# Reordering the last part of the output product and the block loads behind it in a hybrid decoder layer

## The chip, the cores and the metric

One core of a Trainium2 chip runs the whole kernel. The metric is the device time in microseconds of that core for one execution. Five engines work from queues of their own, each in order: PE (matrix products, with its weight loads listed as PEld), DVE (vector operations), ACT (activations, copies and casts), POOL and SP (here used almost only to issue DMAs). An engine waits for another through semaphores.

## The reference, cut to what matters

One layer: a normalised input is projected; a branch of causal pooling and a branch of a state-space scan (SSD) are each multiplied by an output matrix, weighed by sigmoid gates and added; an MLP follows. The change touches the end of the SSD branch (`y_ssd`) and the start of the pooling branch.

```python
def mamba2_branch(z, xbc, dt_raw, conv_w, conv_b, dt_bias, a_log, d_skip, norm_w):
    ...
    y = ssd_chunked(xs, dt, a, b_mat, c_mat) + xs * d_skip[:, None]
    y = y.reshape(bsz, seqlen, D_INNER) * jax.nn.silu(z)
    yg = y.reshape(bsz, seqlen, SSM_GROUPS, D_INNER // SSM_GROUPS).astype(jnp.float32)
    yg = yg * lax.rsqrt(jnp.mean(yg * yg, axis=-1, keepdims=True) + EPS)
    return yg.reshape(bsz, seqlen, D_INNER).astype(z.dtype) * norm_w
...
        y_pool = pool_mixer(u_pool, pool_w_group[i], pool_scale[i]) @ w_pool_up[i]
        y_ssd = mamba2_branch(z, xbc, dt_raw, conv_w[i], conv_b[i], dt_bias[i], a_log[i],
                              d_skip[i], ssd_norm_w[i]) @ w_ssd_out[i]
        h = h + (gate_pool * y_pool + gate_ssd * y_ssd) @ w_o[i]
```

There are 512 tokens, a width of 1024, and 8 groups in the SSD branch with 256 channels each, so 16 slices of 128 channels go into `@ w_ssd_out`.

## The kernel before

**Numbers in two parts.** Every fp32 operand is split into a high part (a cast on ACT) and a low part (a subtraction on DVE), and a product is made of three: high by high, high by low, low by high (`mm3s`, lines 147, 148 and 150). Weights come as blocks of 128x1024: SP loads `raw`, ACT casts `whi`, DVE subtracts `wlo`. There are three `raw` buffers (a fourth here and there while the scan runs) and four each of `whi` and `wlo`, so the load of a block waits until DVE is done with the block three before. Blocks 56 to 67 are the ones that matter here.

**The end of the scan.** `ssd(g)` works through the eight groups. Its last steps for group 7 are: products `po` and `py`, the chain on DVE that makes `yt`, its square `sqg` on ACT (L707), the high part `qhg` (ACT, L331) and the low part `qlg` (DVE, L332) of the sum of squares, two column-sum products `png` on PE (L713, L714), the root `rs` on ACT (L716), reciprocals on DVE, and the split of the result into `yh` and `yl` (L725, L726). Beside it `out_part` runs, piece by piece, as a second generator: eight tiles `psp0` to `psp7` (one for each 128 output channels), each a product with slices 8 to 13 of y. Slices 12 and 13 come from group 6 and are late, so for tiles 0 and 1 they are taken apart (`late`, L884) and go over both tiles in turn. A finished tile is copied out of PSUM by ACT into one of two staging buffers (`sp`, L872), and POOL adds it to `acc_d` in memory by an accumulating DMA (L873). Tiles of `psp` and the pool pair's `pxx` share two PSUM buffers (`psum2`); `png`, `py`, `pz`, `po` and `psl` share four others (`psum1`).

**Behind it.** `pool_pair` makes eight products of the first pool pair from three weights (A, S, D) and a half one (B), with partial sums `pxx`, `py` and `pz` that ACT and DVE copy or add into `pu` between the products (L1012 to L1031). The weights S and D are sums of the raw blocks (`sm`, L986 to L991). Then the last part of the SSD output, slices 14 and 15 of y (group 7), comes in eight tiles `psl0` to `psl7` from two blocks (64 for tiles 0 to 3, 65 for 4 to 7, handed out by `units`), and DVE adds each to `acc` (L1065), which POOL has read back from `acc_d` (L1057). Block 66 holds the pool group's weights and block 67 a gate's; `pool_mix` and its products `pg` with `ph` and `pl` (L974, L975) follow.

**What sets the order.** The program is traced in this order, and a scheduler then places instructions on each engine by priority and readiness. `tc.high_priority(100)` moves what is traced inside it ahead; `tc.issue_after(i)` and the helper `after` keep what is traced inside behind instruction `i` on the same engine, without a semaphore. `block(behind, cast_behind)` gives a block's subtraction and its cast such a place.

## Time and profile before

| | us |
|---|---|
| median of 3 timed runs | 1001.3 (1001.02 to 1001.38) |
| the profiled execution's own time | 999.86 |
| its span, first to last instruction | 998.2 |
| busy time in the span: PE / PEld / DVE / ACT / POOL | 986.7 / 873.1 / 804.1 / 602.0 / 120.1 |

Busy time of PE is pipelined time, so 99% of the span does not say that PE could not be faster; it says that PE hardly ever stands still. Where it does stand still is to be read from the waits of PE and of its weight loads, and from the timeline around them. The `out_part` tiles run from about 430 to 474 us of the span, the first pool pair from 474 to 485, and the `psl` tiles from 485 to 496.

### The profile page before, as it was taken

Reading aid. Unit: us, or ns where it says so; the run is one execution under the profiler, and the core shown is the slowest. Engines: PE = TensorE matmul, PEld = TensorE weight load, DVE = VectorE, ACT = ScalarE, POOL = GpSimd, SP = SyncE. Lnnn points to the kernel's source line nnn. Section 1 sums busy time; section 2 is a strip of 40 time slices with the busy share of each in tenths; the row PEclk is TensorE's granted clock in tenths of the full one; section 3 lists DMA queues with packets and bytes.
Section 4 is the critical chain, followed back from the end, with each engine's and each line's share of the span. In section 5 each row is a group of like instructions: output and inputs, shape, how many; then the busy total and the mean of one; then the engine's idle time right before and its main releaser. Section 6 shows DMA issues by size and latency. Waiting matters only on the chain.

```text
span 998.2 us, 15676 instructions
## 1 busy us (share of the span) xinstructions
PE 986.7 (99%) x6035; PEld 873.1 (87%) x6035; DVE 804.1 (81%) x1162; ACT 602.0 (60%) x855; POOL 120.1 (12%) x216
## 2 busy tenths in 40 slices
PE   8999999999999999999999999999999999999997
PEld 7889998989889999978899888888889999999986
DVE  7978997879845888978789657877988888888885
ACT  8657839495924658574345443378666656656654
POOL 0011321211212212223200022100000000000000
PEclk9999999999999999999999999999999999999999
DMA  7274967667897848678813777864164454464332
GB/s 255 84 257 147 271 196 215 188 194 210 227 274 238 242 124 268 218 159 173 284 67 128 255 247 186 261 177 155 64 190 148 151 187 150 147 188 149 129 106 85
DMA packets 61803, 184.52 MB, mean 185 GB/s; under 512 B 7072, under 2 KB 8416, under 8 KB 60704
## 3 DMA queue, kind: packets, MB, share of 16 engines
q1 hardware_dynamic: 39456, 109.00, 32.9%
q0 software_dynamic: 18240, 67.51, 26.3%
q10 hardware_dynamic: 4032, 7.00, 1.9%
q8 instruction: 47, 0.77, 0.3%
q14 instruction: 28, 0.23, 0.1%
HBM read 173.13 MB, written 58.59 MB: 232 GB/s over the span
## 4 chain that ended last, share of the span: by engine, by line
PE 93%; ACT 3%; DMA 2%; DVE 1%; issue 1%; SPq 0%; ACTq 0%; DVEq 0%
PE px L1468 8%; PE px L216 8%; PE alpha L1536 6%; PE pz L216 6%; PE px L1471 4%; PE px L219 4%; PE alpha L1539 3%; PE pgp L216 3%; PE pz L219 3%; PE pgs L216 3%; PE py L695 2%; PE pqx L510 2%; DMA raw<-in_w 2%; PE pso L147 1%; PE pgp L219 1%; PE wo_alpha L1229 1%
## 5 line engine op out<-in xcount | busy, mean ns | idle before, releaser
L114 DVE TENSOR_TENSOR wlo<-raw,whi 128x1024 fp32r<-128x1024 f32 (+2 forms) x88 | 102.1, 1172 | 37.7 <-ACT whi L112 21.7
L112 ACT CAST whi<-raw 128x1024 fp32r<-128x1024 f32 (+2 forms) x88 | 87.2, 1011 | 67.8 <-PE pso L148 15.3
L216 PE MATMUL px<-uh,whi 128*128 128x264 f32 (+1 forms) x320 | 80.9, 291 | 0.0
L219 PE MATMUL px<-ul,whi 128*128 128x264 f32 (+1 forms) x320 | 78.8, 285 | 0.0
L1243 DVE TENSOR_TENSOR ht<-ht,alpha 128x1024 f32<-128x1024 f32 x35 | 42.7, 1219 | 29.1 <-PE alpha L1536 29.1
L1160 ACT CAST shi<-rawf 128x1024 fp32r<-128x1024 f32 x42 | 44.2, 1053 | 28.7 <-PE alpha L1539 18.2
L216 PEld LDWEIGHTS px<-uh,whi 128*128 128x128 f32 x320 | 60.4, 189 | 0.9 <-issue 0.7
L219 PEld LDWEIGHTS px<-ul,whi 128*128 128x128 f32 x320 | 60.2, 188 | 0.4 <-issue 0.2
L1536 PE MATMUL alpha<-shi,hh 128*128 128x512 f32 x140 | 55.2, 394 | 0.0
L1539 PE MATMUL alpha<-shi,hl 128*128 128x512 f32 x140 | 54.7, 391 | 0.0
L1161 DVE TENSOR_TENSOR slo<-rawf,shi 128x1024 fp32r<-128x1024 f32 x42 | 51.2, 1219 | 0.6 <-ACT shi L1160 0.6
L1471 PE MATMUL px<-vsl,shi 128*128 128x256 f32 x192 | 47.4, 280 | 0.0
L1468 PE MATMUL px<-vsh,shi 128*128 128x256 f32 x192 | 47.4, 281 | 0.0
L216 PE MATMUL pz<-uh,whi 128*128 128x512 f32 x112 | 43.7, 390 | 0.0
L219 PE MATMUL pz<-ul,whi 128*128 128x512 f32 x112 | 43.6, 390 | 0.0
L216 PE MATMUL px<-uh,wlo 128*128 128x264 f32 (+1 forms) x320 | 41.8, 283 | 0.0
L216 PEld LDWEIGHTS px<-uh,wlo 128*128 128x128 f32 x320 | 39.9, 188 | 0.0
L1652 POOL DMA_DIRECT2D fw<-in_fnw x1 | 0.6, 577 | 308.2 <-DVE slo L1161 308.2
L1536 PE MATMUL alpha<-slo,hh 128*128 128x512 f32 x140 | 37.4, 389 | 0.0
L1468 PEld LDWEIGHTS px<-vsh,shi 128*128 128x128 f32 x192 | 36.2, 188 | 0.9
L1471 PEld LDWEIGHTS px<-vsl,shi 128*128 128x128 f32 x192 | 36.1, 188 | 0.9
L1471 PE MATMUL px<-vl,shi 128*128 128x256 f32 x144 | 36.1, 283 | 0.0
(600 smaller groups left out, 3098.8 us busy)
## 6 DMA issues: line engine op xcount, KB each, us to landing
raw<-in_w SPq DMA_DIRECT2D x96, 512.0 KB, 4.6
f_t<-in_f POOLq DMA_DIRECT2D x38, 512.0 KB, 6.5
f_s<-in_f POOLq DMA_DIRECT2D x26, 512.0 KB, 7.0
b<-in_f SPq DMA_DIRECT2D x21, 512.0 KB, 4.5
rawf<-in_f SPq DMA_DIRECT2D x36, 256.0 KB, 2.9
rawf<-f_t SPq DMA_DIRECT2D x36, 256.0 KB, 3.1
abc<-acs_d POOLq DMA_DIRECT2D x8, 1024.0 KB, 7.6
f_t<-f_t POOLq DMA_DIRECT2D x12, 512.0 KB, 5.6
```

The costliest lines, as they stand in the source:

```text
L112: act.copy(hi[:, c], raw[:, c])
L114: dve.tensor_tensor(lo[:, c], raw[:, c], hi[:, c].bitcast(F32), op=ALU.subtract)
L216: pe.matmul(o, wt, rhs[0][k][:, c], start=part == 0 and k == 0, stop=part == 1 and k == NK - 1)
L219: mm[0] = pe.matmul(o, wt, rhs[1][k][:, c], start=False, stop=False)
L510: at = pe.matmul(o, wk, f[k][0], start=start and not low and k == 0, stop=stop and low == 1 and k == 3, skip_group_check=True)
L1160: splits.append((act.copy(hi, src), dve.tensor_tensor(lo, src, hi.bitcast(F32), op=ALU.subtract)))
L1161: dve.tensor_tensor(lo, src, hi.bitcast(F32), op=ALU.subtract)))
L1243: added[0] = dve.tensor_tensor(o, o, src, op=op)
L1468: pe.matmul(ps, m, f[k][0], start=start and not low and k == 0, stop=stop and low == 1 and k == 3, skip_group_check=True)
L1471: pe.matmul(ps, m, f[k][1], start=False, stop=False, skip_group_check=True)
L1536: pe.matmul(ps[t], hh[:, p, seg, st], m, start=bool(first and not low and p == 0), stop=bool(last and low and p == 1), skip_group_check=True)
L1539: pe.matmul(ps[t], hl[:, p, seg, st], m, start=False, stop=False, skip_group_check=True)
```

## The change

There are four edits. (1) The late products of tiles 0 and 1 are made one tile after the other, and each tile's copy (`add`) follows at once, at raised priority. (2) The split of the last group's y is traced at raised priority. (3) The first four additions of `psl` are traced at raised priority. (4) The second block that `units` hands out (block 65) gets its subtraction behind the first addition and its cast behind the copy of `pz` in the first pool pair (`copied`).

```diff
-    def units():
+    def units(behind=tuple):
 
         while True:
-            hi, lo = block()
+            hi, lo = block(*behind())
...
-        for i in range(2):
-            y = yt[:, i, :]
...
+        with tc.high_priority(100) if g == G - 1 else nullcontext():
+            for i in range(2):
+                y = yt[:, i, :]
...
         late = [[(next(un), ys[k]) for k in (12, 13)] for d in range(2)]
-        for o in ((0, 0), (1, 0), (0, 1)):
-            for d in range(2):
+        for d in range(2):
+            for o in ((0, 0), (1, 0), (0, 1)):
                 for n, (a, b) in enumerate(late[d]):
                     pe.matmul(ps[d], a[o[0]], b[o[1]], start=False, stop=o[1] == 1 and n == 1)
+            with tc.high_priority(100):
+                add(ps[d], d)
             yield
-        for d in range(2):
-            add(ps[d], d)
...
-    un = units()
     psl_add = []
+    un = units(lambda: (psl_add[0], copied[POOL_ORDER[0]]) if psl_add else ())
     for d in range(NK):
         ps = psum1(f"psl{d}")
         mm3s(ps, [(next(un), ys[k]) for k in (14, 15)])
-        psl_add.append(dve.tensor_tensor(acc[d], acc[d], ps, op=ALU.add))
+        with tc.high_priority(100) if d < 4 else nullcontext():
+            psl_add.append(dve.tensor_tensor(acc[d], acc[d], ps, op=ALU.add))
```

No instruction is added or taken away on any engine; line numbers move by one or two. What the scheduler makes of it is seen at three places. The first is on ACT, at the copies of tiles 0 and 1 (`sp0`, `sp1`), before:

```order
L648 ACTIVATE abc7_4633<-abc7_4633 128x1024
L850 CAST whi58_4819<-raw58_4818 128x1024
L649 ACTIVATE abc7_4633<-abc7_4633 128x1024
L872 COPY sp0_4811<-psp0_4664 128x512
L872 COPY sp1_4814<-psp1_4665 128x512
L850 CAST whi59_4888<-raw59_4887 128x1024
```

and in the changed kernel:

```order
L648 ACTIVATE abc7_4633<-abc7_4633 128x1024
L873 COPY sp0_4757<-psp0_4664 128x512
L649 ACTIVATE abc7_4633<-abc7_4633 128x1024
L873 COPY sp1_4785<-psp1_4665 128x512
L851 CAST whi58_4810<-raw58_4809 128x1024
L851 CAST whi59_4878<-raw59_4877 128x1024
```

The copy of tile 0 moved ahead of block 58's cast and of the second exponential of the scan's decays (`abc`), and that cast moved behind both copies. The second place is on ACT too, from the last y to the copy of `pz` in the pool pair, before:

```order
L725 CAST yh7_0_4877<-yt7_4755 128x512
L725 CAST yh7_1_4882<-yt7_4755 128x512
L872 COPY sp6_4967<-psp6_4942 128x512
L133 CAST whiS3_5039<-sm3_5032 128x1024
L133 CAST whiD3_5045<-raw62_5028 128x1024
L133 CAST whiB3_5049<-raw63_5030 128x512
L872 COPY sp7_4989<-psp7_4970 128x512
L1012 COPY pu6_5053<-pxx3_5055 128x264
L112 CAST whi64_5177<-raw64_5176 128x1024
L1018 ACTIVATE pu7_5054<-pxx3_5055 128x264
L112 CAST whi65_5215<-raw65_5214 128x1024
L1021 COPY pu7_5054<-pz3_5057 128x264
```

and in the changed kernel:

```order
L873 COPY sp6_4967<-psp6_4942 128x512
L726 CAST yh7_0_4905<-yt7_4760 128x512
L726 CAST yh7_1_4910<-yt7_4760 128x512
L133 CAST whiS3_5039<-sm3_5032 128x1024
L873 COPY sp7_4989<-psp7_4970 128x512
L133 CAST whiD3_5045<-raw62_5028 128x1024
L1013 COPY pu6_5053<-pxx3_5055 128x264
L133 CAST whiB3_5049<-raw63_5030 128x512
L112 CAST whi64_5177<-raw64_5176 128x1024
L1019 ACTIVATE pu7_5054<-pxx3_5055 128x264
L1022 COPY pu7_5054<-pz3_5057 128x264
L112 CAST whi65_5215<-raw65_5214 128x1024
```

The copies of tiles 6 and 7 moved ahead of the last y's casts and of `whiD`, and block 65's cast moved behind the copy of `pz`. The third place is on PE, where the two column-sum products `png` of group 7 stand, before:

```order
L150 MATMUL psp4_4886<-yh5_0_4152,wlo59_4889 128x512
L713 MATMUL png7_4845<-qhg7_4805,ones_r_74 128x512
L150 MATMUL psp4_4886<-yh5_1_4157,wlo59_4889 128x512
L150 MATMUL psp4_4886<-yh6_0_4624,wlo59_4889 128x512
L714 MATMUL png7_4845<-qlg7_4806,ones_r_74 128x512
L150 MATMUL psp4_4886<-yh6_1_4629,wlo59_4889 128x512
L147 MATMUL psp5_4914<-yh4_0_3552,whi59_4888 128x512
```

and in the changed kernel:

```order
L147 MATMUL psp5_4914<-yh4_0_3552,whi59_4878 128x512
L148 MATMUL psp5_4914<-yl4_0_3553,whi59_4878 128x512
L147 MATMUL psp5_4914<-yh4_1_3557,whi59_4878 128x512
L148 MATMUL psp5_4914<-yl4_1_3558,whi59_4878 128x512
L147 MATMUL psp5_4914<-yh5_0_4152,whi60_4916 128x512
L148 MATMUL psp5_4914<-yl5_0_4153,whi60_4916 128x512
L713 MATMUL png7_4867<-qhg7_4839,ones_r_74 128x512
L147 MATMUL psp5_4914<-yh5_1_4157,whi60_4916 128x512
L148 MATMUL psp5_4914<-yl5_1_4158,whi60_4916 128x512
L714 MATMUL png7_4867<-qlg7_4840,ones_r_74 128x512
```

They moved nine matmuls back, from tile 4 into tile 5; on ACT the copy of tile 4 stands between `sqg` and `qhg` now, where it stood behind `rs` before. On DVE the first addition is followed by block 65's subtraction `wlo65`, two additions, `wlo66`, the fourth addition and `wlo67`; before, `wlo65` stood ahead of the pool pair's last copies, and `wlo66` and `wlo67` between the third addition and the fourth. The last addition and the next pair's `wloA` stand ahead of the two `pl` now, and behind them before.

More of the change, by code (lines that the diff above doesn't have):

```diff
@@ L719, in ssd @@
         yield
-        for i in range(2):
-            y = yt[:, i, :]
-            dve.scalar_tensor_tensor(y, y, col(V_SN, 2 * g + i), rs, op0=ALU.mult, op1=ALU.mult)
-            yh = yp.tile([P, SEQ], F32R, tag="yh", name=f"yh{g}_{i}")
-            yl = yp.tile([P, SEQ], F32R, tag="yl", name=f"yl{g}_{i}")
-            act.copy(yh, y)
-            dve.tensor_tensor(yl, y, yh.bitcast(F32), op=ALU.subtract)
-            ys.append((yh, yl))
+        with tc.high_priority(100) if g == G - 1 else nullcontext():
+            for i in range(2):
+                y = yt[:, i, :]
+                dve.scalar_tensor_tensor(y, y, col(V_SN, 2 * g + i), rs, op0=ALU.mult, op1=ALU.mult)
+                yh = yp.tile([P, SEQ], F32R, tag="yh", name=f"yh{g}_{i}")
+                yl = yp.tile([P, SEQ], F32R, tag="yl", name=f"yl{g}_{i}")
+                act.copy(yh, y)
+                dve.tensor_tensor(yl, y, yh.bitcast(F32), op=ALU.subtract)
+                ys.append((yh, yl))
         yield
```

## Prediction

> **What bounds the kernel now.** First the page: the span, and the chain of work that ended last by engine.

> ```profile
> span 998.2 us, 15676 instructions
> PE 93%; ACT 3%; DMA 2%; DVE 1%; issue 1%; SPq 0%; ACTq 0%; DVEq 0%
> ```

> The chain runs on PE for 93% of the span, so only stalls of PE are worth anything, and work on DVE, ACT, SP or POOL counts only where PE waits for it. Next the list of waits, taken for PE's weight loads (PEld), and the busy time by stage: before, inside and after the stretch that the diff touches.

> ```profile
> PEld psp L147 <- ACT sp L872: 1.9, 1, 1.9
> ...
> PEld pz L1005 <- ACT pu L1021: 1.0, 1, 1.0
> ...
> 438.70:485.10 46.40, 43.92 (x257) 37.04 (x257) 35.93 (x57) 24.71 (x37) 14.39 (x21) 1.00 0.81 193
> 485.10:998.20 513.10, 507.62 (x2856) 445.16 (x2854) 416.92 (x548) 287.09 (x413) 22.74 (x37) 1.00 0.51 161
> ```

> The columns of the last two rows are length, then busy time of PE, PEld, DVE, ACT and POOL, the clock (1.00), the DMA share and GB/s. In the 46.40 us of the touched stretch PE is idle for 2.48 us, and two of the largest waits of the whole kernel lie there, one on the copy of a product (`sp`), one on a copy in the pool pair (`pu`). These two are what the change can win. After 485.10 PE stands still for 5.48 of 513.10 us, in crumbs. From there on I assume that everything follows PE, so what PE gains by then reaches the end.

> **The first stall**, from the timeline (start, length, operation, idle time and its releaser in brackets):

> ```profile
> 441.28 0.89 PEld L884 LDWEIGHTS psp<-yl,whi 128*128 128x128 f32 x4
> 444.04 0.19 PEld L147 LDWEIGHTS psp<-yh,whi 128*128 128x128 f32 x1 [1.88 <-ACT sp L872]
> 444.04 0.50 PE L147 MATMUL psp<-yh,whi 128*128 128x512 f32 x1 [1.45 <-ACT sp L872]
> 445.25 1.09 PE L695 MATMUL py<-abc,xdt 128*64 128x128 f32 x14
> 440.57 1.06 ACT L648 ACTIVATE abc<-abc 128x1024 f32<-128x1024 f32 x1
> 441.53 1.04 ACT L850 CAST whi<-raw 128x1024 fp32r<-128x1024 f32 x1
> 442.47 1.05 ACT L649 ACTIVATE abc<-abc 128x1024 f32<-128x1024 f32 x1
> 443.42 1.05 ACT L872 COPY sp<-psp 128x512 f32<-128x512 f32 x2
> ```

> Tile 2 of the product reuses the buffer of tile 0, which ACT copies out only at 443.42, behind a cast and an exponential. Both tiles become ready together, after the twelve late matmuls of L884. In the changed order tile 0 is complete after six of them (before the `po` matmul, about 440.5), and its copy stands where the cast stood, at 441.53. A copy takes 0.59 us (the row at 457.20 below), so it ends at 442.12. PE's last weight load of L884 ends at 442.17, and the same twelve matmuls and the same `po` wait stand before it as now. So the wait goes whole: **-1.88 us**. The exponential at 442.47 comes forward by half a microsecond, since a copy of 0.59 stands before it and no cast. The displaced cast (block 58) ends at about 444.5; tile 2 asks for it only behind eight matmuls with block 57 (0.23 each) and a group of `py`, of which fourteen instructions alone take 1.09: past 445. That hides it; without this cover it would cost the 0.95 by which it is late.

> [...]

> **The second stall** (timeline, then the chain in order of time):

> ```profile
> 479.15 0.65 PE L1005 MATMUL pz<-t1h,wloS 128*128 128x264 f32 x4
> 482.06 0.19 PEld L1005 LDWEIGHTS pz<-t1h,whiB 128*128 128x128 f32 x1 [1.02 <-ACT pu L1021]
> 482.06 0.39 PE L1005 MATMUL pz<-t1h,whiB 128*128 128x264 f32 x1 [0.81 <-ACT pu L1021]
> ...
> 473.92 6.67 DMA raw<-in_w
> ...
> 480.68 1.05 ACT whi L112
> 481.73 0.29 ACT pu L1021
> ```

> ACT takes its queue in order: the cast of block 65 stands ahead of the copy of `pz`, and waits for a load that lands at 480.68, while `pz` had been complete since 479.80. The change queues this cast behind the copy. The product that waits then finds its buffer free: **-1.02 us**.

> **What the change makes late: the column sums.** Tile 4's copy now stands ahead of the cast `qhg` on ACT, and the two `png` matmuls move from inside tile 4 to inside tile 5.

> ```profile
> 457.20 0.59 ACT L872 COPY sp<-psp 128x512 f32<-128x512 f32 x1 [0.35 <-PE psp L150]
> ...
> 459.51 0.62 ACT L331 CAST qhg<-sqg 128x512 fp32r<-128x512 f32 x1 [0.76 <-DVE sqg L708]
> 460.16 0.69 DVE L332 TENSOR_TENSOR qlg<-sqg,qhg 128x512 fp32r<-128x512 f32 x1 [0.69 <-ACT qhg L331]
> 460.37 0.40 PE L713 MATMUL png<-qhg,ones_r 128*128 128x512 f32 x1
> 461.54 0.40 PE L147 MATMUL psp<-yh,whi 128*128 128x512 f32 x1
> 465.72 1.41 DVE L722 SCALAR_TENSOR_TENSOR yt<-yt,vs,rs 128x512 f32<-128x512 f32 x2
> ```

> Tile 5 starts at 461.54; without the two `png` (0.23 each: six such matmuls take 1.52 in a row below, with 0.16 of overhang) and 1.88 earlier that is 459.2, so tile 4 is complete at 459.4. Copy, then `qhg` 0.48 behind it (the spacing of the 457.20 copy and what follows it), which ends at 460.5, 0.4 later than now. PE reaches the first `png` six matmuls after 459.2, at 460.6, and the second three matmuls on, at 461.25; `qlg` would end at 461.2. Both meet within 0.1. Bounds: 0, and 0.7 if `qlg` is hidden by nothing; I take **+0.2**, near the lower one, as the rows meet.

> **The last y and the copies of the pool pair.** The two `yh` casts now stand behind the copy of tile 6, and the copy of tile 7 between `whiS` and `whiD`, so a single file on ACT and DVE leads from tile 6 to the copy that frees the pool pair's first sum:

> ```profile
> 468.36 1.52 PE L150 MATMUL psp<-yh,wlo 128*128 128x512 f32 x6
> 469.96 0.59 ACT L872 COPY sp<-psp 128x512 f32<-128x512 f32 x1 [2.17 <-PE psp L150]
> 466.51 1.28 ACT L725 CAST yh<-yt 128x512 fp32r<-128x512 f32 x2
> 468.43 0.69 DVE L986 TENSOR_TENSOR sm<-raw,raw 128x512 f32<-128x512 f32 x1
> 469.15 0.69 DVE L988 TENSOR_TENSOR sm<-sm,raw 128x512 f32<-128x512 f32 x1
> 470.44 1.05 ACT L133 CAST whiS<-sm 128x1024 fp32r<-128x1024 f32 x1
> 471.39 1.05 ACT L133 CAST whiD<-raw 128x1024 fp32r<-128x1024 f32 x1
> 475.46 0.38 ACT L1012 COPY pu<-pxx 128x264 f32<-128x264 f32 x1 [0.82 <-PE pxx L1005]
> 476.70 0.28 PE L1005 MATMUL pxx<-t0h,whiS 128*128 128x264 f32 x1
> ```

> Count from T, the end of tile 6 (469.88 now, about 468.2 then). The copy starts at T+0.08, `yh` 0.48 later at T+0.56. From the start of `yh` to the end of the second `sm` are 469.84 - 466.51 = 3.33, so `whiS` starts at T+3.9, the copy of tile 7 at T+4.85, `whiD` at T+5.33, the copy of `pxx` at T+6.28, and it ends at T+6.66. PE needs it at 476.70 - 469.88 = T+6.82. (`yt` is ready: 467.13 now, about 0.3 later then, still before T.) So it just fits: **+0.1**, between 0 and 1.0 should a link slip. Behind it nothing of the pair is short: its next copies wait for PE alone.

> **The additions.** DVE now does the first four additions and blocks 65 to 67 in alternation; the addition of tile 7, `wloA` and `wlo65` (0.6 + 1.14 + 1.14 by their spacing) move ahead of the last `pl`:

> ```profile
> 487.12 0.68 DVE L1065 TENSOR_TENSOR acc<-acc,psl 128x512 f32<-128x512 f32 x1
> ...
> 497.23 1.29 DVE L975 TENSOR_TENSOR pl<-pu,ph 128x512 fp32r<-128x512 f32 x2
> 502.06 0.39 PE L148 MATMUL pg<-pl,whi 128*128 128x512 f32 x1
> ```

> The second `pl` ends at 498.52 now; 2.6 earlier and 2.9 later is 498.8. PE asks at 502.06 - 2.6 = 499.5. 0.65 us of cover are left: **0**, and at most 0.5 if the DVE gains less than PE. Of the DMAs, SP issues the same loads in the same order; POOL's read of `acc0` now stands behind tile 6's store, about 1 us after T, and has until its reader, the addition at 487.12 - 2.6 = 484.5.

> **Sum.** -1.88 - 1.02 + 0.2 + 0.1 = -2.6 us. The profiled execution then has a span of 995.6 and, with the 1.66 around it, takes 997.3 and not 999.86. The runs shown have a median of 1001.3, 1.44 above the profiled one; the same difference gives **998.7 us**, 0.26% less. About 0.2% (2.0 us) is what a measurement here tells from no change, so I call less than 999.3 faster. Ends of the terms: -2.9, and -2.9 + 0.7 + 1.0 + 0.5 = -0.7.

> **Rivals.** (a) *The stall moves.* If the file behind tile 6 slips by 1 to 1.5 us, PE stands in front of the pool pair's second product instead. A place for it: staging tiles are two, so tile 6's copy needs tile 4's store landed, and the store's time is the one link that varies:

> ```profile
> DMA to landing us min/median/max: 3.8/5.7/9.3
> ```

> For it: a margin of 0.16. Against it: every other link is a row, and that store, issued behind the copy that ends at 460.0, has 8 us, against a median of 5.7 for the stores of `sp`; only the longest would bite, by 1.2. -2.6 + 1.2: 999.9, within 0.2%.

> (b) *Only the matmul idles count*, because a weight load behind a wait costs nothing of its own. For it: PE's row shows 1.45 of idle time, not 1.88. Against it: the loads of both places start with the release. PE's own idle time at `pz` is 0.81. -1.45 - 0.81 + 0.3 = -1.96: 999.3, on the border. [...]

> (c) *Not what it says.* The early copy has no effect, if tile 0's sum is complete no earlier. Against: its last matmul stands before `po`. Then only the 1.02 is won, 1000.4.

> (d) *Slower: the second block's loads.* Blocks 65, 66 and 67 load into the buffers that `wloD`, `wloB` and `wlo64` free, which come up to 2 us later, and DVE in its order waits for their casts before it finishes `pl`.

> ```profile
> DMA to landing us min/median/max: 3.5/5.9/8.9
> ```

> This is the row of the tile `raw` in the touched stretch, whose DMA share is 0.81. From its first addition at 484.5 DVE comes to `wlo67` behind four additions (0.6 each), `wlo65` and `wlo66` (1.14 each): 489.2. Its load is issued when `wlo64` is done, which I put at 478, and a cast of 1.05 follows it; so with the cover of 0.65 the load may take 10.8 us. Beyond that every microsecond is PE's. To be slower by over 0.2% it must take 15 us (2.6 + 2.0 over the 10.8): 1003.3 and more. Against it: 8.9 at most now.

> **How the numbers follow.** Forecast 0.65 (998.0 to 999.3), (a) 0.12, (b) 0.08, (c) 0.05, (d) and its like 0.10. Faster: the forecast and half of (b), 0.69. Within 0.2%: (a), (c), half of (b) and 0.01 of (d)'s small cases, 0.22. Slower 0.09. The range takes the forecast, (a), (b) and (c): 998.0 to 1000.6.

> **What would show it.** Right: no wait of PEld on `sp` at tile 2 and none on `pu` in front of `pz`; the first `psl` matmul near 482.4 and not 485.06; the stretch after it as long as now. Wrong: a PEld wait on `qhg`/`qlg` or on the `pxx` copy above 0.5, DVE waiting for a cast before `wlo66` or `wlo67`, or `pg` waiting for `pl`.

## The result, and the profile after

Six executions of the changed kernel took 996.60 to 997.72 us, median 997.21. The kernel before, run beside it, took 999.33 to 999.81; with the three executions shown first its median is 1000.41. The ratio is 0.9969, 95% interval 0.9959 to 0.9979: faster by 0.2 to 0.4%. The forecast was 998.7 in a range of 998.0 to 1000.6, so the direction was right and the time lies below the range. The profiled execution took 997.27 us, with a span of 995.6; the sum had said 997.3 and 995.6.

The page and the list of waits of the changed kernel (weight loads of PE, the same view as before):

```profile
span 995.6 us, 15677 instructions
PE 96%; ACT 2%; DVE 1%; DMA 0%; issue 0%; ACTq 0%; DVEq 0%
```

```profile
PEld po L689 <- DVE st L677: 1.2, 2, 1.0
...
PEld pg L148 <- DVE pl L976: 0.7, 2, 0.4
...
PEld png L713 <- ACT qhg L331: 0.3, 1, 0.3
...
PEld png L714 <- DVE qlg L332: 0.2, 1, 0.2
```

Both waits that the change was to remove (1.9 on `sp`, 1.0 on `pu`) are gone from the list. Two new ones stand there that the prediction named: `png`, and `pg` waiting for `pl`. The busy time by stage shows where the gain lies (columns as before: length, PE, PEld, DVE, ACT, POOL, clock, DMA share, GB/s):

```profile
438.70:482.50 43.80, 43.59 (x258) 36.83 (x257) 34.61 (x55) 21.96 (x34) 16.15 (x24) 1.00 0.84 199
482.50:995.60 513.10, 507.63 (x2853) 444.60 (x2851) 417.74 (x549) 289.29 (x415) 21.05 (x33) 1.00 0.51 162
```

The touched stretch has shrunk from 46.40 to 43.80 us, PE's idle time in it from 2.48 to 0.21. That what follows is 513.10 us long in both is due to where it is cut: 482.50 lies half a microsecond behind the first `psl` matmul. Cut at that matmul in both kernels (485.06 and 481.99), the stretch is 3.07 shorter and what follows 0.47 longer, and the two waits for `pl` lie there. The timeline (start, length, operation, idle time and its releaser in brackets), first ACT at tiles 0 and 1, then PE's weight loads and two rows of PE:

```profile
441.29 0.56 ACT L873 COPY sp<-psp 128x512 f32<-128x512 f32 x1
441.75 1.06 ACT L649 ACTIVATE abc<-abc 128x1024 f32<-128x1024 f32 x1
442.71 0.57 ACT L873 COPY sp<-psp 128x512 f32<-128x512 f32 x1
```

```profile
441.49 0.42 PEld L885 LDWEIGHTS psp<-yl,whi 128*128 128x128 f32 x2
441.96 0.19 PEld L147 LDWEIGHTS psp<-yh,whi 128*128 128x128 f32 x1
...
460.28 0.19 PEld L713 LDWEIGHTS png<-qhg,ones_r 128*128 128x128 f32 x1 [0.30 <-ACT qhg L331]
461.01 0.19 PEld L714 LDWEIGHTS png<-qlg,ones_r 128*128 128x128 f32 x1 [0.20 <-DVE qlg L332]
...
498.73 0.19 PEld L148 LDWEIGHTS pg<-pl,whi 128*128 128x128 f32 x1 [0.42 <-DVE pl L976]
499.33 0.19 PEld L148 LDWEIGHTS pg<-pl,whi 128*128 128x128 f32 x1 [0.30 <-DVE pl L976]
...
457.52 1.52 PE L150 MATMUL psp<-yh,wlo 128*128 128x512 f32 x6
481.99 0.39 PE L147 MATMUL psl<-yh,whi 128*128 128x512 f32 x1
```

Tile 0's copy starts at 441.29 (the prediction had 441.53), and tile 2's first weights load at 441.96, right behind the late products. Against the kernel before, PE runs ahead by 0.24 at the first late product (438.52 against 438.76, before anything the change touches), by 2.16 in tile 4 (457.52 against 459.68), 2.00 from the second half of tile 5 to the pool pair's products, 3.07 at the first `psl` matmul (481.99 against 485.06), and 2.6 from the second pair's products to the end.

### The profile page after: what moved, and what is told of

Its sections match the earlier page's. It is cut to its first block, busy times and chain, and to the rows that moved or that the text cites. A ratio compares the mean times of both kernels' runs of the same rounds, so it can differ in the third digit from the quotient of the medians.

```text
span 995.6 us, 15677 instructions
## 1 busy us (share of the span) xinstructions
PE 987.4 (99%) x6035; PEld 873.0 (88%) x6035; DVE 803.7 (81%) x1162; ACT 601.7 (60%) x855; POOL 119.6 (12%) x216
## 4 chain that ended last, share of the span: by engine, by line
PE 96%; ACT 2%; DVE 1%; DMA 0%; issue 0%; ACTq 0%; DVEq 0%
PE px L1470 8%; PE px L216 8%; PE alpha L1538 6%; PE pz L216 6%; PE px L1473 4%; PE px L219 4%; PE alpha L1541 3%; PE pgp L216 3%; PE pz L219 3%; PE pgs L216 3%; PE pqx L510 2%; PE py L695 2%; PE pxx L1006 2%; PE po L689 2%; PE pso L147 2%; PE pgp L219 1%
## 5 line engine op out<-in xcount | busy, mean ns | idle before, releaser
L112 ACT CAST whi<-raw 128x1024 fp32r<-128x1024 f32 (+2 forms) x88 | 87.2, 1011 | 68.9 <-PE pso L148 15.3
```

Of the source, the lines that this page charges most:

```text
L112: act.copy(hi[:, c], raw[:, c])
```

## Experiments

Fourteen profiles show how executions differ before the edits matter: the first late product starts anywhere between 438.44 and 439.79. So kernels are compared below by the stretch from that matmul to the first product of the first `pgs` gate, which all edits lie in, and by the times. From that gate's first product to the end of the span all fourteen take 473.6 to 473.8 us. So what PE gains by then reaches the end, as the prediction assumed, and the spans of two profiles differ only by their start and by this stretch:

| kernel | stretch, us | time: median (lowest to highest), executions | kernel before beside it | ratio, 95% |
|---|---|---|---|---|
| before (first profile) | 85.72 | | | |
| before (`b0`) | 85.36 | 1000.49 (999.33 to 1001.38), 11 | 1000.21 | 0.9991 to 1.0009 |
| before (`b1`) | 86.97 | 1000.83, 1 | 999.83 | |
| the change (first profile) | 83.39 | 997.21 (996.60 to 997.72), 6 | 1000.41 | 0.9959 to 0.9979 |
| the change (`a0`) | 82.93 | 997.48 (996.88 to 998.93), 7 | 1000.28 | 0.9963 to 0.9984 |
| the change (`a1`) | 82.97 | 997.97 (996.92 to 1001.50), 12 | 999.83 | 0.9971 to 0.9989 |
| edit 1 alone (`e1`) | 88.24 | 1002.06 (1000.88 to 1002.66), 11 | 1000.28 | 1.0003 to 1.0021 |
| edit 4 alone (`e4`) | 86.25 | 1000.20 (998.85 to 1001.29), 11 | 1000.28 | 0.9987 to 1.0004 |
| change without edit 3 (`no3`) | 87.72 | 1001.49 (999.78 to 1002.45), 11 | 1000.28 | 1.0000 to 1.0018 |
| change without edit 4 (`no4`) | 85.95 | 1000.60 (999.49 to 1001.52), 11 | 1000.21 | 0.9994 to 1.0012 |
| change without edit 1 (`no1`) | 84.71 | 999.32 (999.03 to 1000.32), 11 | 999.83 | 0.9986 to 1.0004 |
| before, filler products (`fill`) | 85.21 | 999.89 (998.96 to 1000.33), 11 | 1000.21 | 0.9983 to 1.0003 |
| change, qhg ahead (`c1`) | 84.01 | 999.11 (997.87 to 999.92), 11 | 1000.21 | 0.9976 to 0.9993 |
| change, wloA behind pl (`r2`) | 84.95 | 999.20 (998.00 to 1000.38), 11 | 999.83 | 0.9982 to 0.9999 |

### Is the difference the kernel's, and one part or several?

The changed kernel unaltered (`a0`):

> The changed kernel, unaltered, against the kernel before. Theory (the difference of 2.6 us is the kernel's, and the 1.4 to 1.7 us between the two sets of runs of the kernel before, 1001.0 to 1001.4 and 999.3 to 999.8, belong to the chip or the session): inside this one call the runs of each kernel agree within 0.5 us, and the changed one is 2.4 to 2.8 us below the kernel before, at whatever level that one stands. Rival (the two levels are states that the kernel before falls into from one execution to the next, and the change rids it of the upper one): inside this call the runs of the kernel before spread over 1 us or more, while the changed one stays within 0.5.

Measured: 2.80 below, at 997.48. But the kernel before, on one chip and side by side with it, spread from 999.00 to 1001.98, and the changed one, in six of seven executions, over 0.75 (the seventh lies 1.3 above them). So the two levels (999.3 to 999.8, 1001.0 to 1001.4) are no matter of the chip. The theory fell; the rival is right about the kernel before, though its 0.5 for the changed one was not met. The question was what the kernel before falls into.

Edit 1 alone (`e1`):

```diff
-        for o in ((0, 0), (1, 0), (0, 1)):
-            for d in range(2):
+        for d in range(2):
+            for o in ((0, 0), (1, 0), (0, 1)):
...
+            with tc.high_priority(100):
+                add(ps[d], d)
```

> Edit (1) alone. On ACT this also puts the copy of the pool pair's second sum ahead of block 65's cast, as in the whole change; but DVE's subtraction for block 65 now stands ahead of DVE's addition of that sum. Theory (edits 3 and 4 are needed to keep DVE free of block 65): both stalls of PE on ACT go (-1.9 and -1.0, +0.2 for the column sums), DVE waits for block 65's cast until about 484.8 and is about 2 us later with the pool pair than in the kernel before, so 1 to 2 us come back as PE's waits on an addition or on pl: 1.0 to 2.0 us below the kernel before. Rival (edits 3 and 4 give nothing): 2.4 us or more below it. Second rival (edit 1 touches the first stall only): the PE weight load in front of pz still waits about 1.0 for ACT, 1.7 below.

Edit 4 alone (`e4`):

```diff
-            hi, lo = block()
+            hi, lo = block(*behind())
...
+    un = units(lambda: (psl_add[0], copied[POOL_ORDER[0]]) if psl_add else ())
```

> Edit (4) alone. Theory: the whole idle time of the weight load in front of pz goes (-1.0), nothing comes back: span 1.0 below the kernel before, first stall (1.9 on sp) untouched. Rival (only the matmul's idle time counts): 0.8 below. Rival (PE does not gain, since block 65's cast and subtraction, now later, are waited for by psl or pl): 0 to 0.5 below.

The change without edit 3 (`no3`) and without edit 4 (`no4`):

```diff
-        with tc.high_priority(100) if d < 4 else nullcontext():
+        with nullcontext():
```

> The change without edit (3), the raised priority of the first four additions: on DVE the pool averages and both pl now stand ahead of the last addition and of wloA. Theory (the 0.45 us that PE gives back in front of pg comes from DVE's order, wlo67 waiting for its late load and wloA ahead of pl): PE's waits on pl fall from 0.7 to at most 0.2, and the kernel is 0.3 to 0.5 below the whole change. Rival (edit 3 is what frees the psl buffers in time): a PE wait on an addition appears, and it is 0.3 or more above the whole change. Rival (the 0.45 is the load of block 67 itself): same as the whole change within 0.2.

```diff
-    un = units(lambda: (psl_add[0], copied[POOL_ORDER[0]]) if psl_add else ())
+    un = units()
```

> The change without edit (4): on ACT nothing moves, on DVE block 65's subtraction stands ahead of the addition of the pool pair's second sum. Theory (edit 4 is needed: DVE waits there for block 65, which lands about 483.5): the addition of the second sum comes about 5 us later than in the whole change, the averages and the first psl additions behind it too, PE waits 2 us or more in front of psl for an addition, and the kernel is 2 to 5 us above the whole change. Rival (the early copy on ACT is enough, and edit 4's subtraction is hidden): within 0.3 of the whole change.

Measured: edit 1 alone is 1.8 us slower than the kernel before, where 1.0 to 2.0 faster was expected, though both old stalls are gone from its profile. Its list of waits, PE's weight loads:

```profile
PEld psl L147 <- DVE acc L1065: 2.6, 2, 2.1
PEld psl L147 <- ACT whi L112: 2.4, 1, 2.4
PEld psl L147 <- DVE pu L1027: 0.9, 1, 0.9
```

Its rows on DVE, ACT, SP's queue and PE's weight loads:

```profile
479.82 0.43 DVE L1024 TENSOR_TENSOR pu<-pu,pxx 128x264 f32<-128x264 f32 x1 [1.79 <-PE pxx L1005]
485.53 1.23 DVE L114 TENSOR_TENSOR wlo<-raw,whi 128x1024 fp32r<-128x1024 f32 x1 [5.28 <-ACT whi L112]
486.67 0.42 DVE L1027 TENSOR_TENSOR pu<-pu,pz 128x264 f32<-128x264 f32 x1
484.44 1.05 ACT L112 CAST whi<-raw 128x1024 fp32r<-128x1024 f32 x1 [5.78 <-DMA raw<-in_w]
475.98 2.40 SPq L96 DMA_DIRECT2D raw<-in_w  x3
...
489.95 0.68 DVE L1065 TENSOR_TENSOR acc<-acc,psl 128x512 f32<-128x512 f32 x1
490.75 0.19 PEld L147 LDWEIGHTS psl<-yh,whi 128*128 128x128 f32 x1 [2.38 <-ACT whi L112]
```

and the same row of SP's queue in the kernel before:

```profile
473.92 5.16 SPq L96 DMA_DIRECT2D raw<-in_w  x3
```

DVE stands in front of block 65's subtraction for 5.28 us, since that block's cast starts at 484.44 and not at 480.68. The loads of blocks 65 to 67 wait for buffers that DVE now frees later: the first is issued at 475.98 and not at 473.92, the three of them within 2.40 and not 5.16 us. That is 2.06 of the 3.76; the rest passes between issue and landing, and no run here shows why. Behind the subtraction in DVE's queue are the addition that frees `pz` and all `psl` additions, and PE waits 5.9 us for them. The list puts 2.4 of this down to ACT's cast of block 67, which ends at 490.60. But the load that waits there is the first of `psl4`, which needs nothing of that block: it reuses the buffer of `psl0`, and the first addition, which frees it, ends at 490.63, just before the load starts. The theory named the place; it expected 1 to 2 us of such waits.

Without edit 4 the same wait is there:

```profile
484.38 1.23 DVE L114 TENSOR_TENSOR wlo<-raw,whi 128x1024 fp32r<-128x1024 f32 x1 [4.51 <-ACT whi L112]
488.81 0.68 DVE L1067 TENSOR_TENSOR acc<-acc,psl 128x512 f32<-128x512 f32 x1
489.60 0.19 PEld L147 LDWEIGHTS psl<-yh,whi 128*128 128x128 f32 x1 [2.33 <-ACT pu L1032]
```

The addition of the pool pair's second sum comes 4.7 us later than in the change, and the first `psl` addition behind it ends at 489.49. PE waits 2.33 for it, again at `psl4`: the view names the copy of `pxx`, which ends 0.03 later, but `psl4` uses neither that copy nor its buffer. PE also waits 1.3 for `pl`, and the stretch is 2.6 to 3.0 longer than the change's. So the theory was right in size and in mechanism. Without edit 3 my theory fell, and its rival won by far more than it asked: 4.0 above the change, side by side. PE's and DVE's rows of `no3`:

```profile
492.66 0.19 PEld L147 LDWEIGHTS psl<-yh,whi 128*128 128x128 f32 x1 [3.28 <-DVE acc L1067]
491.30 0.71 DVE L964 TENSOR_TENSOR pw<-pu 128x527 f32<-128x527 f32 x1 [3.38 <-ACT pu L1032]
491.93 0.68 DVE L1067 TENSOR_TENSOR acc<-acc,psl 128x512 f32<-128x512 f32 x1
```

Without edit 3 a pool average (`pw`) stands ahead of the second addition. It waits for ACT's last copy of `pxx`, which stands behind block 67's cast, which waits for that block's load. PE then waits 3.28 us for a buffer that only the addition frees. (Part of the 4.0 is the clock: in this profile it is halved for 3.4 us behind the wait, and the four executions of `no3` with a mean clock of 0.999 or more lie 2.3 to 3.3 above the change.)

Edit 4 alone took 1.0 of the second stall away (no weight load waits in front of its `pz` any more), yet its median is the kernel before's: 4 of 11 executions lie at 998.85 to 999.46 with a mean clock of 0.999 or 1.000, the others at 1000.05 to 1001.29 with 0.997 or 0.998, the profiled one among these. (The mean clock is the clock granted to PE over an execution, as a share of full speed.) Its profile led to the cause of the two levels.

(Edit 2 moved nothing: the kernel without it has the same instructions in the same order on all engines. The last y's casts come to stand where they do through edit 1, as `e1`'s profile has them in the same place.)

### Where the two levels come from

In `e4`'s profile the granted clock is 0.50 for over three microseconds behind the first stall. Three things tested whether that is the upper level: products that fill the stall (`fill`), the change with the old tiles 0 and 1 (`no1`, edit 1 undone), and more profiles of the kernel before.

```diff
+        with tc.high_priority(100):
+            for _ in range(6):
+                pe.matmul(full[1][:, SEQ:], late[1][0][0][0], late[1][0][1][0], start=True, stop=True)
         for d in range(2):
             add(ps[d], d)
```

> The kernel before, with six products of 128x512 more on PE between the last late product of tile 1 and the first of tile 2 (about 1.4 us of work, into the unused half of tile 1's PSUM buffer, read by nobody): PE works through most of the first stall, which keeps its length. Theory (the upper of the two levels of the kernel before, about 1001.2 against 999.9, is the granted clock, halved for about 3 us behind the first stall in some executions): with PE busy the clock stays up, all runs lie near the lower level, 999.5 to 1000.3, none at a mean clock of 0.998 or less, and the median falls by 0.3 to 0.8. Rival (the two levels are something else, a load or the start): both levels stay, some third of the runs above 1000.9 and the median as before, within 0.2. Rival (the filler products themselves delay tile 2): all runs 0.3 or more above the lower level.

> The change without edit (1): tiles 0 and 1 as in the kernel before, everything behind the pool pair as in the change. Theory (first stall 1.9 and, in a third or more of the executions, some 1.5 us of halved clock behind it; second stall 1.0): two levels as in the kernel before, the lower near 998.9, the upper near 1000.3, median 0.7 to 1.2 below the kernel before, and 1.5 to 2.6 above the whole change. Rival (the upper level comes from the pool pair or the psl tiles): one level, near 998.9, spread below 1 us.

> The kernel before, unaltered, for more of its executions beside each other and one more profile. Theory of the clock: two levels, about 1.3 us apart, the upper one with a mean clock of 0.998 or less; if the profiled execution is one of the upper level, the granted clock is near 0.5 for about 3 us behind the first stall (444 to 449), the fourteen py products there take about 1.9 and not 1.09, and the rest of the span is as in the first profile. Rival: an upper-level profile shows full clock there, and its loss elsewhere.

> The kernel before, for one more profile. Theory of the clock: if its time is above 1000.8, the granted clock is near 0.5 for some 3 us behind the first stall and nowhere else between 30 and 950 us; if it is below 1000.3, the clock there is full. Rival: a time above 1000.8 with full clock there.

Measured: `b1` is an execution of the upper level. Its windows around the first stall, then PE's row of the products that follow (1.09 long in the kernel before's first profile):

```profile
442.10:445.51 3.41, 1.97 (x16) 1.25 (x17) 3.41 (x5) 3.41 (x6) 1.54 (x2) 1.00 0.11 6
...
445.40:445.80 0.40, 0.40 (x9) 0.40 (x6) 0.40 (x1) 0.40 (x1) 0.37 (x1) 0.64 1.41 102
...
446.60:448.40 1.80, 1.80 (x7) 1.61 (x8) 1.80 (x3) 0.00 (x0) 0.00 (x0) 0.50 1.07 139
...
448.80:449.00 0.20, 0.20 (x2) 0.16 (x1) 0.20 (x1) 0.00 (x0) 0.00 (x0) 0.69 0.93 266
```

```profile
443.73 0.50 PE L147 MATMUL psp<-yh,whi 128*128 128x512 f32 x1 [1.44 <-ACT sp L872]
...
444.94 1.45 PE L695 MATMUL py<-abc,xdt 128*64 128x128 f32 x14
...
447.77 0.63 PE L147 MATMUL psp<-yh,whi 128*128 128x512 f32 x1
```

The column before the DMA share is the clock: 0.64 in a window of 0.40 us, taken as a mean of 1.00 and 0.50, the values of the rows around it, means that 28% of it passed at 1.00 and the rest at 0.50, so the drop begins at 445.51; 0.69 in the other puts its end at 448.92. For these 3.41 us the granted clock is 0.50 (a 128x512 matmul of `psp` takes 0.63 and not 0.40), and by the end of it PE has lost 1.59 us against the first profile: the first late product is 0.32 earlier, the first product of tile 2 behind the drop 1.27 later. Of this 1.25 is left in the stretch of the table, since the second stall is 0.7 us in `b1` and not 1.0. `e4` shows the same drop from 445.5 to 448.9; the first profile and `b0` show a clock of 1.00 there. Between 30 and 950 us no other window of `b1` has a clock below 1.00. `b0`'s time of 1000.49 lies between the levels because of its start, 1.0 us later than the first profile's. Of `b0`'s own eleven executions four lie above 1000.7, all with a mean clock of 0.998.

With the stall filled (`fill`), this is the row:

```profile
444.74 0.19 PEld L147 LDWEIGHTS psp<-yh,whi 128*128 128x128 f32 x1 [0.52 <-ACT sp L872]
```

PE waits only 0.52 for `sp`, and none of 11 executions lies above 1000.33, while 12 of the 33 beside them lie above 1000.7. The median fell by 0.3, the low end of what was expected, and by itself not clear of no change (0.9983 to 1.0003). One detail of the expectation missed: two of the 11 have a mean clock of 0.998. One of them is the profiled one, and its clock is 1.00 behind the first stall (440 to 452 us) and 0.96 from 950 us to the end (by that mean, an estimate of some 4 us at 0.50). So the mean clock of one execution isn't made here alone. `no1`, which keeps the stall, has two levels again, eight executions at 999.03 to 999.59 and three at 1000.28 to 1000.32, though with a median 0.5 and not 0.7 below the kernel before, and 1.35 and not 1.5 above the change. Its mean clocks do not separate the levels: 0.997, 0.998 and 1.000 in the upper three, 0.998 in three of the lower eight. Over the three sets that ran beside the experiments, 33 of 91 executions of the kernel before lie above 1000.7, and 29 of these 33 have a mean clock of 0.998 or less, against 4 of the other 58. With the six executions of the first result, the medians of the two groups are 999.75 and 1001.18: 1.43 apart. For four of the 33 the mean clock shows no such fall.

### Two versions meant to be better

`c1` keeps the copies of tiles 4 to 7 behind `qhg`, to take the cost of the column sums back; `r2` keeps the next pair's `wloA` and `sm` behind both `pl`.

```diff
-            add(ps, d)
+            add(ps, d, halved.get(G - 1) if d >= 4 else None)
```

> The change, and in addition the copies of tiles 4 to 7 kept behind the cast qhg on ACT, so that qhg starts when its sum is ready (about 458.3) and not behind tile 4's copy (459.6). Theory (the column sums cost 0.16 to 0.2 in the change): PE's waits of 0.3 and 0.2 in front of png go, tile 5's second half starts 2.1 to 2.2 before that of the kernel before and not 2.0, and the kernel is 0.1 to 0.4 below the whole change. Rival (the split of the last y, one cast of which moves behind tile 6's copy again, makes the pool pair's weights late): PE waits in front of the pool pair, no gain or a loss.

```diff
-    nxt = pool_pair(POOL_ORDER[1], psl_add[:2])
+    nxt = pool_pair(POOL_ORDER[1], (lows_[0], lows_[0]), lows_[0])
```

> The change, and in addition block A of the next pool pair (its subtraction wloA, and the sums sm) kept behind both pl on DVE. Theory (the 0.45 given back in front of pg is DVE's order: wlo67 late with its load, and wloA of 1.14 ahead of pl): pg waits for pl no longer, 0 to 0.45 below the whole change, the rest of the span as it. Rival (the next pair's weights then come late): PE waits in front of that pair's products, same or slower than the whole change. Rival (pl is bound by ph on ACT and by the last average, not by wloA): the wait for pl stays above 0.3.

> The changed kernel, unaltered, once more beside the kernel before. Theory: 2.4 to 3.2 us below the median of the kernel before (996.9 to 997.6), no run near an upper level; PE's wait for pl in front of pg between 0 and 0.7, as block 67's load falls. Rival (the first result was a lucky session): less than 2 us below.

Measured: both are slower than the change, `r2` by 1.2 side by side, `c1` by its stretch (84.01 against 82.93 to 83.39), as it was not timed beside the change. Each has the wait that its rival named. In `c1` the waits in front of `png` are gone, and PE waits in front of the pool pair's second product:

```profile
470.45 0.59 ACT L874 COPY sp<-psp 128x512 f32<-128x512 f32 x1 [2.44 <-DMA acc_d<-sp]
470.93 0.62 ACT L726 CAST yh<-yt 128x512 fp32r<-128x512 f32 x1
476.46 0.19 PEld L1007 LDWEIGHTS pxx<-t0h,whiS 128*128 128x128 f32 x1 [0.72 <-ACT pu L1014]
```

and from its chain of work, tile 4's store:

```profile
461.46 8.89 DMA acc_d<-sp
```

Measured from the first late product, tile 4's copy is no later than in the change (20.56 us behind it, against 20.61). But POOL now issues a load of 512 KB (`f_s`) ahead of tile 4's store: in the change the store is issued at 460.01 and that load at 460.94, in `c1` the load at 460.93 and the store at 461.46. The store takes 8.89 us to land; in the change no store of `sp` took more than 5.6. So tile 6's copy waits for the staging buffer, and the file on ACT behind it (the last y, `whiS`, `whiD`, the copy of `pxx`) ends 0.72 too late. That the load ahead is why the store takes so long is likely and not shown. In `r2` no load waits for `pl`, and a copy of the second pair and the weights of the third come late instead:

```profile
PEld pxx L1009 <- ACT whiD L133: 0.9, 1, 0.9
PEld pxx L1009 <- ACT pu L1016: 0.6, 1, 0.6
...
PEld pxx L1009 <- DVE wloD L135: 0.4, 1, 0.4
```

There is nothing to repair in most executions anyway: neither `a0`'s profile nor `a1`'s has a load that waits for `pl`. `a1`, at 1.86 below the kernel before, missed the 2.4 expected, and by its own condition, less than 2, the rival came true. The kernel before had fewer upper executions there, 8 of 29. Against its lower ones alone the change gains 1.7 us beside `a1`, 2.4 beside `a0` and 2.5 in the first result. Of `a1`, eleven of twelve executions lie at 996.92 to 998.82, the twelfth at 1001.50, with a mean clock of 0.997 and no profile to say where. Its profile has the touched stretch as short as `a0`'s, and a start that is 1.2 us longer. No version beat the change.

## Where the prediction was right, and the step that failed

**The step that failed** is the last of the sum: "The runs shown have a median of 1001.3, 1.44 above the profiled one; the same difference gives 998.7". I took 1.44 as an offset between profiled and timed executions. It is the distance of two levels of the kernel before (1.43 by 97 executions), and the three shown were, by their times, all of the upper one; their clocks are not on record. That level is half a clock behind the first stall, as `b1` shows in the kernel before itself (0.50 for 3.41 us) and `fill` by taking it away (none of 11 executions above 1000.33). The change removes the stall and this with it: up to 1.59 us more than the -1.88 counted. The sum held for an execution of the lower level (997.3 forecast, 997.27 measured); from the upper level the same change is worth some 4 us. By the stretch the change gains 2.0 to 2.8 us against the two profiles without the drop, and 3.6 to 4.0 against `b1`. The range had no term for it, so its low end of 998.0 excluded what happened. I could have seen that 1.44 of 1000 needs a cause, as the profiled execution's time lay outside the three others.

**The first stall**, -1.88: the lead of PE grew by 1.92 from the first late product to tile 4. Right in mechanism and size. **The second stall**, -1.02: 1.07, from 2.00 to 3.07. Right for the profile that it was read from; that this one was among the long ones is luck, as the same wait is 0.6 in `b0` and 0.7 in `b1`. And it took edits 3 and 4 to keep the gain, which the prediction had counted as moves that cost nothing. What they are worth is 4.0 us (`no3`, by medians taken side by side, part of it the clock) and 2.6 to 3.0 (`no4`, by the stretch): with the first stall gone, the loads and subtractions of blocks 65 to 67 come later while PE comes earlier.

**The column sums**, +0.2: 0.16, with the two waits that were named. **The file behind tile 6**, +0.1: nothing; PE's lead is 2.00 on both sides of it, the copy of `pxx` ending just in time. How narrow that is, `c1` shows: rival (a) with its place, the staging buffer, came true as soon as tile 4's store took 8.89 us to land.

**The additions**, 0 (at most 0.5): 0.45 in the first profile, none in `a0` and `a1`. The mechanism is rival (d)'s in small, and two of the signs named for "wrong" are there: DVE waits for block 67's cast, and `pg` waits for `pl`. In the first profile ACT and DVE meet block 67 like this:

```profile
488.58 1.05 ACT L112 CAST whi<-raw 128x1024 fp32r<-128x1024 f32 x1 [1.40 <-DMA raw<-in_w]
489.67 1.23 DVE L114 TENSOR_TENSOR wlo<-raw,whi 128x1024 fp32r<-128x1024 f32 x1 [0.63 <-ACT whi L112]
497.99 1.28 DVE L976 TENSOR_TENSOR pl<-pu,ph 128x512 fp32r<-128x512 f32 x2
```

In `a0` there is no wait for `pl`, and DVE waits 0.23 for that cast. The price set for it (10.8 us of load covered) was about right: `wlo64` ends at 477.58 and the cast starts 11.0 later, which costs 0.45; in `a0` it starts 10.4 later (477.64 to 488.00), which costs nothing. That the span came out at 995.6 to the tenth owes something to chance: 0.24 of an earlier start against 0.45 here.

**Rival (b)**, that only the matmuls' idle time counts, would have given 1.45 and 0.81; 1.92 and 1.07 were measured, so PE's whole wait is won: in the kernel before the load itself waits, idle for 1.88 until 444.04. **Rival (c)** is excluded by the copy at 441.29.

## What to carry to other kernels

A stall of PE cost twice here: its own length (1.88), and in some executions a clock of 0.50 for 3.41 us behind it (1.59 lost in `b1`), which a single profile may not contain; where timed executions fall into two levels, look for the granted clock behind the largest stall before a difference is put on the median. Measure from one early instruction to a late one, too: here the start of an execution alone moves the time by up to 1.35 us, almost as much as the fall of the clock does. Removing the stall moved PE ahead of loads that were on time before (5.9 us of waits in `e1`): count who frees the buffer of each load behind it, and keep work that waits for a load out of the queues (ACT, DVE) on which PE's buffers are freed. Edits that look like bookkeeping can be what keeps the gain, which only taking them out one at a time tells.
